# Constant loads of GpSimd begun behind the sixth K tile of the first weight block

## The chip, the cores and the metric

The kernel runs on one core of one Trainium2 chip. A core has a matrix engine (TensorE, PE in the profile), three other compute engines (VectorE = DVE, ScalarE = ACT, GpSimd = POOL), a queue engine (SyncE = SP) and 16 DMA engines that all queues share. SP, ACT and POOL can each start transfers; the profile lists what they issue under SPq, ACTq and POOLq, and the transfers themselves under queues q1 (SP), q10 (ACT) and q0 (POOL). The metric is the device time of one execution in microseconds; 2070.61 us is the median of three runs before the change (2067.7 to 2071.45).

## What is computed

Two layers over a sequence of 512 tokens with 2048 features, in float32. Each layer is x + W_out(mixer(RMSNorm(x)) * silu(gate)). The first mixer is gated differential attention with 8 heads, the second a gated RWKV-7 time mixing. Only the first layer's beginning matters here:

```python
hn = rms_norm(x, norm_w[0])
proj = hn @ w_in                                   # 2048 -> 4 * 2048
q, k, v, gate = jnp.split(proj, 4, axis=-1)
q = apply_rope(rms_norm(q, q_gain), cos, sin)      # cos, sin from positions and 64 frequencies
k = apply_rope(rms_norm(k, k_gain), cos, sin)
lam = exp(sum(lam_q1 * lam_k1)) - exp(sum(lam_q2 * lam_k2)) + lambda_init
o = causal_diff_attention(q, k, v, lam)
o = rms_norm(o, subln_w) * (1.0 - lambda_init)     # the output norm, its weights are "subw"
```

So the attention layer needs nine small constants beside its matrices: the positions, the 64 frequencies, two gains of 128, four lambda vectors of 128 and the output norm's 256 weights.

## The kernel before

A float32 product is made of three products of a faster 32-bit type. An operand a is split into hi (a rounded copy) and lo (a - hi), and a*b is hi*hi + hi*lo + lo*hi (`mm3`, L122). For weights ScalarE makes the hi part `wh` (L105) and VectorE the lo part `wl` (L106) of a tile `wraw` of two K tiles by 512 columns, 512 KB (`split_w`). For the input, ScalarE makes `hH` (L1110) and VectorE `hL` (L1111) of one K tile of x transposed, 256 KB, scaled with the norm weights (`make_h`). There are 16 K tiles of 128, so 8 weight tiles in a block of 512 columns.

The first weight block is the Q and K columns of head 0. `unit_tok` goes over its 8 weight tiles; for each it splits the weights, then the two tiles of x (`turn`, which appends the two instructions to `g.made`), and issues 24 products: 4 row tiles of 128 tokens, 2 K tiles, 3 products. Its raw weights have three buffers, wh and wl two each, so the cast of a weight tile waits until TensorE is done with the tile two before it. SP loads x tiles and weight tiles in one fixed order, each issue also waiting for the transfer eight issues before. Weights and x of K tiles 0 to 5 are issued ahead of everything. The second block is the V and gate columns of head 0 (`vg_cols`), with the same `unit_tok`.

Beside these products, VectorE and ScalarE do more: sums of the input tiles for later heads (`input_sums`, L497 to L521, also on tiles named pair), the squares of x for the norm (L888, from 1 MB loads that ScalarE issues at L882 once hH of K tiles 7, 10 and 15 is made), and the constants of the attention layer. The constants are made by `rope_tables` (L195 to L225: positions cast to float at L197, angles at L201, sine and cosine at L211 and L212, tables with the gains at L221 to L225), `lambda_full` (L234 to L243) and the two lines for `subw` (L905, L907). Their nine loads are issued by GpSimd. Each engine works its instructions off in order.

The order of the instructions on each engine is set by a scheduler of the language: it places them by data dependences, by priority (`high_priority`), and by explicit edges: `with tc.issue_after(ins)` puts instructions of the same engine behind `ins`. Before the change, rope_tables stands behind the split of the tenth K tile on ScalarE and VectorE (`g.made[9]`) and, on GpSimd, behind the causal mask (`masked`). So VectorE's and ScalarE's parts have their place in the middle of the first block, while GpSimd's loads start as soon as the mask is made.

Of the kernel before, what the change touches and what calls it, by code (L numbers as in the profile page):

```python
# [13 lines left out]
F32 = mybir.dt.float32  # L14
# [9 lines left out]
P = 128  # L24
# [221 lines left out]
def copy_out(g, dst, ps):  # L246
    with g.tc.high_priority(offset=AHEAD):
        for d, p in zip(dst, ps):
            m = g.nc.scalar.copy(d, p[:])
    return m.ins  # L250
# [562 lines left out]
def layer0(g, aps):  # L813
    nc, tc = g.nc, g.tc
    lx = ExitStack()
    g.lc = lx.enter_context(tc.tile_pool(name="lc0", bufs=1))
    with ExitStack() as cx:
# [56 lines left out]
        copied = copy_out(g, [t[:] for t in t1s], qk0)  # L874
        sc = g.work.tile([P, NT, 4], F32, name="ssc", tag="y", bufs=1)
        for cb, tags in enumerate((("qkL",), ("sA2",), ("sC2",), ("qkL",))):
# [8 lines left out]
            for t in range(NT):  # L885
                junk = g.work.tile([P, 512], F32, name="junkx", tag="al", bufs=1)
                with tc.issue_after(g.made[12 + t][0] if cb == 0 else copied):
# [8 lines left out]
        nc.gpsimd.memset(g.mask[:], 0.0)  # L896
        masked = nc.gpsimd.affine_select(out=g.mask[:], in_=g.mask[:], compare_op=ALU.is_ge, fill=NEG,
                                base=(NT - 1) * P, pattern=[[-1, T]], channel_multiplier=1).ins
        with tc.issue_after(g.made[9][0]), tc.issue_after(g.made[9][1]):
            with tc.issue_after(masked):  # L900
                rope_tables(g, aps)
        with tc.issue_after(copied), tc.issue_after(g.made[-1][1]), tc.issue_after(masked):
            lambda_full(g, aps)
        g.subw = g.lc.tile([P, 2], F32, name="subw")
        nc.gpsimd.dma_start(out=g.subw[:], in_=aps["da_subln_w"][0].rearrange("(c p) -> p c", p=P))  # L905
        with tc.issue_after(g.made[9][1]):
            nc.vector.tensor_scalar(g.subw[:], g.subw[:], 0.5 * (1.0 - LAMBDA_INIT), None, ALU.mult)  # L907
        before = None
        for h in range(NH):
# [850 lines left out]
@with_exitstack  # L1760
def body(ctx, tc, nc, aps):
    g = Ctx()
    g.nc, g.tc = nc, tc
    g.last, g.first, g.centred = None, [], None
    g.chains, g.later, g.state, g.copied = [], [], None, None
    g.const = ctx.enter_context(tc.tile_pool(name="const", bufs=1))
    g.hp = ctx.enter_context(tc.tile_pool(name="hp", bufs=16))
    g.wraw = ctx.enter_context(tc.tile_pool(name="wrawp", bufs=3))
    g.wh = ctx.enter_context(tc.tile_pool(name="whp", bufs=2))
    g.wl = ctx.enter_context(tc.tile_pool(name="wlp", bufs=2))  # L1770
    g.small = ctx.enter_context(tc.tile_pool(name="small", bufs=2))
    dr = ctx.enter_context(tc.tile_pool(name="dr", bufs=1, space=DRAM))
    g.ys = [dr.tile([D - 256, T], F32, name=f"ys{i}") for i in range(2)]
    g.yd2 = dr.tile([D, T], F32, name="yd2")
    g.xd = aps["x1"] if "x1" in aps else dr.tile([T, D], F32, name="xd")
    g.ltd = dr.tile([2, 2, 2, NC_, HALF + 1, HALF], F32, name="ltd")
    g.td = dr.tile([2, HALF // NG, P, HALF], F32, name="td")
    g.ident = g.const.tile([P, P], F32, name="ident")
    make_identity(nc, g.ident)
    for n, layer in ((4, layer0), (2, layer1)):  # L1780
        with tc.tile_pool(name="pp", bufs=n, space=PSUM) as g.pp, \
                tc.tile_pool(name="ps", bufs=1, space=PSUM) as g.ps:
            layer(g, aps)
# [41 lines left out]
```

## Time and profile before

| | |
|---|---|
| median of three runs | 2070.61 us (2067.7 to 2071.45) |
| profiled execution | 2071.26 us |
| its span | 2069.6 us |
| TensorE busy | 2050.2 us, 99% |
| VectorE busy | 1610.9 us, 78% |
| ScalarE busy | 1129.7 us, 55% |
| GpSimd busy | 389.0 us, 19% |
| DMA, whole span | 297.76 MB, 144 GB/s |

Times in the profile count from the span's start. A row of the timeline is start, length, engine, line, operation, out<-in, count, and in brackets how long the engine had been idle and what ended that. Issues of transfers have the engine's name with a q; what lands is seen where an engine stops waiting for it. Matmuls overlap: a product of 512 columns is shown 0.39 us long while the next one starts well before it ends. PEclk is the granted clock of TensorE as a share of full speed.

### The profile page before, as it was taken

The numbers are of one execution on the slowest core, as the hardware profiler recorded it, in microseconds if no ns is written. First come the engines' busy times: TensorE is split into PE (matmuls) and PEld (weight loads), VectorE is DVE, ScalarE is ACT, GpSimd is POOL, SyncE is SP. The second block draws the span as 40 slices with busy tenths as digits, with TensorE's granted clock in tenths as the row PEclk, the third lists the DMA queues.
The fourth block names the chain that finished last, engine by engine and source line by source line (L and its number), as shares of the span: only waits on it lengthen the run. The fifth ranks groups of instructions, "written<-read, shape, count | busy, mean of one in ns | idle before, by whom it ended". The sixth has DMA issues, their size and how long they took to land.

```text
span 2069.6 us, 34177 instructions
## 1 busy us (share of the span) xinstructions
PE 2050.2 (99%) x11936; PEld 1676.1 (81%) x11936; DVE 1610.9 (78%) x4121; ACT 1129.7 (55%) x2246; POOL 389.0 (19%) x773
## 2 busy tenths in 40 slices
PE   9999999999999999999999999999999999999999
PEld 7888888888888888888777778888888888877787
DVE  6988989888898976475778887877778878777755
ACT  4765666566665544345465555555555555545333
POOL 1010211102111100101122222222222222232011
PEclk9999999999999999999999999999999999999999
DMA  8487978879787965733323233233333332346676
GB/s 269 133 182 193 167 186 182 169 189 164 186 179 173 255 234 166 173 91 107 102 82 93 84 92 96 78 103 100 97 97 92 89 97 80 110 129 202 197 193 142
DMA packets 159533, 297.76 MB, mean 144 GB/s; under 512 B 64528, under 2 KB 81936, under 8 KB 159360
## 3 DMA queue, kind: packets, MB, share of 16 engines
q1 hardware_dynamic: 110768, 184.39, 28.6%
q0 software_dynamic: 25952, 90.88, 23.2%
q10 hardware_dynamic: 22640, 20.30, 3.0%
q8 instruction: 94, 1.54, 0.3%
q14 instruction: 79, 0.65, 0.1%
HBM read 271.33 MB, written 24.18 MB: 143 GB/s over the span
## 4 chain that ended last, share of the span: by engine, by line
PE 87%; DVE 8%; ACT 2%; issue 2%; DMA 2%; ACTq 0%; DVEq 0%; POOLq 0%; SPq 0%
PE pp L122 44%; PE pp L573 22%; PE pt L122 5%; DVE wl L106 2%; PE sm L1514 2%; PE gp L1324 1%; PE sc L122 1%; PE o L122 1%; PE sm L1532 1%; PE sm L1525 1%; PE lora L122 1%; PE z L122 1%; PE Y L1554 1%; ACT wh L105 1%; DMA wraw<-in_da_w_in_dram 1%
## 5 line engine op out<-in xcount | busy, mean ns | idle before, releaser
L106 DVE TENSOR_TENSOR wl<-wraw,wh 128x1024 fp32r<-128x1024 f32 (+2 forms) x290 | 355.2, 1225 | 180.5 <-ACT wh L105 175.5
L105 ACT CAST wh<-wraw 128x1024 fp32r<-128x1024 f32 (+2 forms) x290 | 302.6, 1043 | 260.5 <-PE pp L122 117.6
L122 PE MATMUL pp<-hL,wh 128*128 128x512 f32 x1024 | 414.2, 405 | 0.0
L122 PE MATMUL pp<-hH,wl 128*128 128x512 f32 x1024 | 413.0, 403 | 0.0
L122 PE MATMUL pp<-hH,wh 128*128 128x512 f32 x1024 | 412.7, 403 | 0.0
L122 PEld LDWEIGHTS pp<-hH,wh 128*128 128x128 f32 x1024 | 193.0, 189 | 34.7 <-issue 0.4
L122 PEld LDWEIGHTS pp<-hL,wh 128*128 128x128 f32 x1024 | 193.1, 189 | 33.7
L122 PEld LDWEIGHTS pp<-hH,wl 128*128 128x128 f32 x1024 | 193.3, 189 | 32.3
L573 PE MATMUL pp<-wh,hH 128*128 128x512 f32 x448 | 176.8, 395 | 0.0
L573 PE MATMUL pp<-wh,hL 128*128 128x512 f32 x448 | 175.8, 392 | 0.0
L122 PE MATMUL pp<-wh,hH 128*128 128x512 f32 x376 | 148.2, 395 | 1.9 <-ACT hH L1110 1.7
L122 PE MATMUL pp<-wh,hL 128*128 128x512 f32 x376 | 148.7, 395 | 0.3 <-DVE hL L1111 0.2
L122 PE MATMUL pp<-wl,hH 128*128 128x512 f32 x376 | 148.1, 394 | 0.7 <-DVE wl L106 0.5
L1383 DVE SCALAR_TENSOR_TENSOR tmpl<-LT,Tm 128x60 f32<-128x60 f32 (+24 forms) x496 | 134.1, 270 | 13.3
L573 PE MATMUL pp<-wl,hH 128*128 128x512 f32 x448 | 140.3, 392 | 0.0
L1520 POOL COPY SA<-VS 64x64 f32<-64x64 f32 x224 | 57.1, 255 | 401.7 <-DVE VS L1536 381.4
L1385 DVE TENSOR_TENSOR Tm<-Tm,tmpl 128x60 f32<-128x60 f32 (+24 forms) x496 | 104.0, 210 | 11.7
L1517 ACT COPY rhs<-sm 64x64 f32<-64x64 f32 x256 | 53.0, 207 | 91.2 <-PE sm L1514 88.7
L573 PEld LDWEIGHTS pp<-wl,hH 128*128 128x128 f32 x448 | 84.4, 188 | 17.2
L573 PEld LDWEIGHTS pp<-wh,hH 128*128 128x128 f32 x448 | 84.2, 188 | 17.2 <-issue 0.3
L573 PEld LDWEIGHTS pp<-wh,hL 128*128 128x128 f32 x448 | 84.2, 188 | 16.2
L1527 ACT COPY VS<-sm 64x64 f32<-64x64 f32 x256 | 52.9, 206 | 72.0 <-PE sm L1525 65.6
(403 smaller groups left out, 4381.8 us busy)
## 6 DMA issues: line engine op xcount, KB each, us to landing
wraw<-in_rw_w_in_dram SPq DMA_DIRECT2D x128, 512.0 KB
wraw<-in_da_w_in_dram SPq DMA_DIRECT2D x75, 512.0 KB
wraw<-in_da_w_in_dram POOLq DMA_DIRECT2D x28, 512.0 KB, 6.7
wraw<-in_da_w_out_dram SPq DMA_DIRECT2D x26, 512.0 KB
wraw<-in_rw_w_out_dram SPq DMA_DIRECT2D x24, 512.0 KB
Ta<-in_da_w_in_dram POOLq DMA_DIRECT2D x21, 512.0 KB, 5.8
Tb<-in_da_w_in_dram POOLq DMA_DIRECT2D x21, 512.0 KB, 5.8
Tc<-in_da_w_in_dram POOLq DMA_DIRECT2D x21, 512.0 KB, 5.5
```

Of the source, the lines that this page charges most:

```text
L105: a = nc.scalar.copy(hi[:, ks], raw[:, ks])
L106: d = nc.vector.tensor_sub(lo[:, ks], raw[:, ks], hi[:, ks].bitcast(F32))
L122: m = nc.tensor.matmul(out, a, b, start=s, stop=e, skip_group_check=skip)
L573: m = nc.tensor.matmul(out[t][:], x, wt[lo][:, k, :], start=first, stop=end and lo == 1 and k == KG - 1, skip_group_check=True)
L1324: m = nc.tensor.matmul(gp[h][:, i * P : (i + 1) * P], BK[r_, c0 + i, :, :], p.AR[r_, c0 + i, :, :], start=True, stop=True)
L1383: nc.vector.scalar_tensor_tensor(tt, LT[:, i : i + 1, i + 1 :].to_broadcast([P, s, n]), n2[:, i : i + 1], Tm[:, 0:s, i : i + 1].to_broadca ...
L1385: nc.vector.tensor_add(Tm[:, 0:s, i + 1 :], Tm[:, 0:s, i + 1 :], tt)
L1514: nc.tensor.matmul(sm[:, 0:P], both(p.G[:, c, 0]), both(VS[:, c]), start=True, stop=True)
L1517: nc.scalar.copy(rhs[r_, :], sm[r_, h * C : h * C + C])
L1520: nc.gpsimd.tensor_copy(p.SA[r_, c - 1, :], VS[r_, c, h, :])
L1525: nc.tensor.matmul(sm[:, P : P + C], both(g.TT[j % 2][:, c]), rhs[:], start=True, stop=True)
L1527: g.copied = nc.scalar.copy(VS[r_, c, h, :], sm[r_, P : P + C])
```

## The change

GpSimd gets one more instruction, a copy of one column of `hL[5]` into a small tile that nothing reads. hL[5] is the lo part of the sixth K tile, made by VectorE. The name `masked` now stands for this copy, so everything that stood behind the mask on GpSimd, which is the loads of rope_tables and of lambda_full, stands behind the copy; the load of the output norm's weights is put behind it too. The scale of those weights on VectorE (0.5 * (1 - lambda_init)) no longer stands behind K tile 9 but behind the last K tile.

```diff
         masked = nc.gpsimd.affine_select(out=g.mask[:], in_=g.mask[:], compare_op=ALU.is_ge, fill=NEG,
                                 base=(NT - 1) * P, pattern=[[-1, T]], channel_multiplier=1).ins
+        behind = g.small.tile([P, 1], F32, name="behind", tag="so")
+        with tc.issue_after(masked):
+            masked = nc.gpsimd.tensor_copy(behind[:], g.hL[5][:, 0:1].bitcast(F32)).ins
         with tc.issue_after(g.made[9][0]), tc.issue_after(g.made[9][1]):
             with tc.issue_after(masked):
                 rope_tables(g, aps)
         with tc.issue_after(copied), tc.issue_after(g.made[-1][1]), tc.issue_after(masked):
             lambda_full(g, aps)
         g.subw = g.lc.tile([P, 2], F32, name="subw")
-        nc.gpsimd.dma_start(out=g.subw[:], in_=aps["da_subln_w"][0].rearrange("(c p) -> p c", p=P))
-        with tc.issue_after(g.made[9][1]):
+        with tc.issue_after(masked):
+            nc.gpsimd.dma_start(out=g.subw[:], in_=aps["da_subln_w"][0].rearrange("(c p) -> p c", p=P))
+        with tc.issue_after(copied), tc.issue_after(g.made[-1][1]):
             nc.vector.tensor_scalar(g.subw[:], g.subw[:], 0.5 * (1.0 - LAMBDA_INIT), None, ALU.mult)
```

Line numbers behind the change are four higher from L899 on, so L1111 is L1115.

GpSimd's queue at the start of the program, before (the names: ident and mask are made on GpSimd itself, ropein holds the frequencies and the gains, lam the lambda vectors, Ta is the first accumulating weight load of head 1; in brackets the semaphores waited for):

```order
L897 AFFINE_SELECT mask<-mask 128x512 [waits Pool_49]
L195 DMA pos_i<-in_positions_dram 128x4x1
L199 DMA ropein<-in_inv_freq_dram 128x64
L219 DMA ropein<-in_da_q_gain_dram 128x128
L219 DMA ropein<-in_da_k_gain_dram 128x128
L234 DMA lam<-in_da_lam_q_dram 128x128
```

and now:

```order
L897 AFFINE_SELECT mask<-mask 128x512 [waits Pool_49]
L901 COPY behind<-hL 128x1 [waits DVE_49]
L195 DMA pos_i<-in_positions_dram 128x4x1
L199 DMA ropein<-in_inv_freq_dram 128x64
L219 DMA ropein<-in_da_q_gain_dram 128x128
L219 DMA ropein<-in_da_k_gain_dram 128x128
L234 DMA lam<-in_da_lam_q_dram 128x128
```

The loads keep their order; ahead of them there is now a copy that waits for VectorE.

VectorE behind K tiles 8 and 9 of the first block, before (hL here are those two tiles, pos is the cast of the positions):

```order
L106 TENSOR_TENSOR wl<-wraw,wh 128x1024
L1111 SCALAR_TENSOR_TENSOR hL<-pair,norms,hH 128x512 x2
L197 CAST pos<-pos_i 128x4
L907 TENSOR_SCALAR subw<-subw 128x2
L514 TENSOR_SCALAR pair<-pair,norms 128x256
L201 TENSOR_SCALAR rope<-ropein,pos 128x64 x4
```

and now:

```order
L106 TENSOR_TENSOR wl<-wraw,wh 128x1024
L1115 SCALAR_TENSOR_TENSOR hL<-pair,norms,hH 128x512 x2
L197 CAST pos<-pos_i 128x4
L514 TENSOR_SCALAR pair<-pair,norms 128x256
L201 TENSOR_SCALAR rope<-ropein,pos 128x64 x4
```

The two instructions that need the positions and the frequencies keep their place; the scale of subw has left it.

VectorE ahead of the split of the second weight tile of the V and gate block (the L106 row; L502, L514, L519 and L521 are input_sums), before:

```order
L519 SCALAR_TENSOR_TENSOR pair<-pair,norms 128x256
L521 TENSOR_TENSOR pair<-pair 128x256
L514 TENSOR_SCALAR pair<-pair,norms 128x256 x2
L502 SCALAR_TENSOR_TENSOR pair<-pair,norms 128x256 x2
L514 TENSOR_SCALAR pair<-pair,norms 128x256
L106 TENSOR_TENSOR wl<-wraw,wh 128x1024
L502 SCALAR_TENSOR_TENSOR pair<-pair,norms 128x256
L514 TENSOR_SCALAR pair<-pair,norms 128x256
```

and now:

```order
L519 SCALAR_TENSOR_TENSOR pair<-pair,norms 128x256
L521 TENSOR_TENSOR pair<-pair 128x256
L502 SCALAR_TENSOR_TENSOR pair<-pair,norms 128x256
L514 TENSOR_SCALAR pair<-pair,norms 128x256 x2
L502 SCALAR_TENSOR_TENSOR pair<-pair,norms 128x256 x2
L106 TENSOR_TENSOR wl<-wraw,wh 128x1024
L514 TENSOR_SCALAR pair<-pair,norms 128x256
L502 SCALAR_TENSOR_TENSOR pair<-pair,norms 128x256
```

Counted from the first block on, one L502 more stands ahead of this split. SP's order is the same in both kernels; TensorE's differs in the place of two groups of transposes in the second block by one product each; ScalarE's differs by a few instructions of input_sums and an earlier issue of one 32 KB load (mu).

## The prediction

> **What bounds the kernel now.** I read the page first, then the first 30 us in windows, then the chain of waits, then the DMA queues in two stretches. The profiled execution took 2071.26 us with a span of 2069.6 us, 0.65 us above the median of 2070.61 us, and the sum below is made against it.
>
> ```profile
> span 2069.6 us, 34177 instructions
> PE 2050.2 (99%) x11936; PEld 1676.1 (81%) x11936; DVE 1610.9 (78%) x4121; ACT 1129.7 (55%) x2246; POOL 389.0 (19%) x773
> ```
>
> TensorE is busy 99% of the span. A gap of TensorE that closes is therefore worth its length, wherever it lies, provided that nothing opens behind it. The change touches the first weight block, so its gaps are looked at there. Columns: stretch and its length, busy us of each engine, granted TensorE clock, DMA share, GB/s.
>
> ```profile
> 0.00:5.00 5.00, 3.10 (x14) 3.11 (x15) 0.06 (x1) 1.87 (x3) 4.31 (x13) 1.00 0.60 182
> 5.00:10.00 5.00, 4.87 (x22) 3.75 (x21) 2.80 (x5) 3.00 (x5) 2.74 (x5) 1.00 1.03 288
> 10.00:15.00 5.00, 4.80 (x18) 2.85 (x17) 2.73 (x3) 1.58 (x3) 0.00 (x0) 1.00 0.95 132
> 15.00:20.00 5.00, 4.38 (x19) 3.26 (x18) 0.00 (x0) 0.63 (x1) 0.00 (x0) 1.00 0.89 233
> 20.00:25.00 5.00, 3.61 (x10) 2.43 (x11) 3.09 (x4) 3.26 (x6) 0.00 (x0) 0.83 1.02 397
> ```
>
> From 10 to 20 us the DMA engines are busy nine tenths of the time and yet move 132 and 233 GB/s, where the next stretch moves 397. The chain of waits says who suffers:
>
> ```profile
> 4.78 14.49 DMA wraw<-in_da_w_in_dram
> 19.37 1.05 ACT wh L105
> ```
>
> The weight tile of K tiles 4 and 5 is issued at 4.78 us and lands only at 19.3 us. The DMA queues tell why: first the stretch 7 to 19 us, then 19.4 to 37 us (q0 is GpSimd's queue, q1 SP's, q10 ScalarE's; last the share of 16 engines' time).
>
> ```profile
> DMA packets 1047, 2.15 MB, mean 179 GB/s; under 512 B 241, under 2 KB 241, under 8 KB 1047
> ...
> q0 software_dynamic: 265, 0.43, 49.7%
> q1 hardware_dynamic: 782, 1.72, 43.5%
> ...
> DMA packets 2716, 6.54 MB, mean 372 GB/s; under 512 B 270, under 2 KB 270, under 8 KB 2715
> ...
> q1 hardware_dynamic: 2132, 5.39, 79.2%
> q10 hardware_dynamic: 572, 1.14, 19.7%
> ```
>
> GpSimd's nine constant loads bring 0.43 MB and hold half of the DMA engines' time for 12 us, 6.0 us of all sixteen; SP's stream brings 1.72 MB in the remaining 43.5%, at 330 GB/s of its own time. Those 6.0 us stand ahead of a tile that TensorE waits for.
>
> **The change, part by part.** TensorE's own rows give what can be won (the first row is ScalarE's, ahead of the first product). Columns: start, length, engine, line, operation, count, and in brackets the idle time before it.
>
> ```profile
> 5.76 0.72 ACT L1110 ACTIVATE hH<-pair,norms 128x512 fp32r<-128x512 f32 x1 [0.54 <-DMA norms<-in_norm_w_dram]
> ...
> 12.23 0.39 PE L122 MATMUL pp<-wh,hL 128*128 128x512 f32 x1
> 15.11 0.39 PE L122 MATMUL pp<-wh,hH 128*128 128x512 f32 x1
> 18.99 0.39 PE L122 MATMUL pp<-wh,hL 128*128 128x512 f32 x1
> 21.09 0.49 PE L122 MATMUL pp<-wh,hH 128*128 128x512 f32 x1 [1.71 <-ACT hH L1110]
> 29.15 0.39 PE L122 MATMUL pp<-wh,hH 128*128 128x512 f32 x1
> ```
> ```profile
> 23.50:26.50 3.00, 3.00 (x9) 2.34 (x8) 0.50 1.03 400
> 12.71:21.09 8.38, 6.57 (x25) 4.27 (x25) 1.00 0.93 234
> 21.09:29.15 8.06, 7.76 (x25) 5.74 (x25) 0.79 1.03 397
> ```
>
> Each pair of K tiles is 24 products (4 row tiles, 2 K tiles, 3 products). Undisturbed they follow each other every 0.228 us: 17 steps from 15.11 to 18.99. A pair is then 5.47 us. The last product of the first pair starts at 12.23, so the second pair could start at 12.46, the third at 17.93 and the fourth at 23.40. They start at 12.71, 21.09 and 29.15. The loss is 0.25 us before the second pair, 8.38 - 5.47 = 2.91 in it, and 8.06 - 5.47 = 2.59 in the third, 5.75 us together. Of the 2.59 about 1.5 come from the granted clock, 0.50 in the window 23.5 to 26.5: at half clock three microseconds do the work of one and a half.
>
> (a) Removed from the start: the nine loads. With 6.0 us of engine time gone, the tile of K tiles 4 and 5 lands at 13.3 us at the latest (19.3 - 6.0; SP's rate left as it is). At the earliest, with 0.91 MB moved by 5 us (182 GB/s) and 372 GB/s after that, the 2.62 MB up to this tile (4 x tiles of 256 KB, 3 weight tiles of 512 KB) are there at 5 + 1.71/0.372 = 9.6 us. Either will do: ScalarE's cast cannot begin before 12.5, when TensorE gives the weight buffer of the first pair back, and even 13.3 leaves the third pair four microseconds. I take the whole 5.75 us; the lower bound is 4.2, if the slow clock of 1.5 us stays, and the upper 6.3, if the norm weights, for which the first split waits 0.54 us, come that much sooner.
>
> (b) Moved: the nine loads begin behind hL[5]. GpSimd's queue holds nothing else before the accumulating loads of L86 at 110 us, so all that waits behind the new copy are the loads themselves; who waits for them is VectorE, at four places.
>
> ```profile
> 2.36 0.93 POOL L195 DMA_DIRECT2D pos_i<-in_positions_dram  x1
> 3.28 0.57 POOL L199 DMA_DIRECT2D ropein<-in_inv_freq_dram  x1
> 19.37 1.04 ACT L105 CAST wh<-wraw 128x1024 fp32r<-128x1024 f32 x1 [5.43 <-DMA wraw<-in_da_w_in_dram]
> 21.59 1.41 DVE L1111 SCALAR_TENSOR_TENSOR hL<-pair,norms,hH 128x512 fp32r<-128x512 f32 x2
> 30.43 1.22 DVE L106 TENSOR_TENSOR wl<-wraw,wh 128x1024 fp32r<-128x1024 f32 x1 [3.42 <-ACT wh L105]
> 33.30 0.74 DVE L201 TENSOR_SCALAR rope<-ropein,pos 128x64 f32<-128x64 f32 x4
> ```
> ```profile
> ropein<-in_inv_freq_dram POOLq DMA_DIRECT2D x1, 32.0 KB, 6.1
> pos_i<-in_positions_dram POOLq DMA_DIRECT2D x1, 2.0 KB, 6.4
> lam<-in_da_lam_k_dram POOLq DMA_DIRECT2D x2, 64.0 KB, 12.4
> subw<-in_da_subln_w_dram POOLq DMA_DIRECT2D x1, 1.0 KB, 11.6
> L1520 POOL COPY SA<-VS 64x64 f32<-64x64 f32 x224 | 57.1, 255 | 401.7 <-DVE VS L1536 381.4
> ```
>
> From cast to the end of hL[5] is 3.63 us (19.37 to 23.00), so hL[5] is done at 16.1 to 16.9. GpSimd's copy of one column is not in the trace; its nearest row, 64x64, takes 0.26 us, and between nothing and twice that it does not matter. The frequencies landed 7.0 us after the first issue began (0.92 to their own issue, then 6.1): now at 23.4 to 24.2. VectorE wants them at L201, which moves from 33.30 to 27.6, since VectorE's work there hangs on TensorE freeing a weight buffer (the cast behind the third pair). Margin 3.4 us or more, cost nothing. With the landing of the slowest quoted load, 12.4 us, they would come at 29.7 to 30.5, 2.9 us late at most: the lower end. The gains, lambda and norm weights are wanted 9 us and more after L201 and issue within 5 us, so they are covered.
>
> (c) Reordered: VectorE is full from 30 us to 62 us, and TensorE meets that once.
>
> ```profile
> 58.32 0.48 DVE L502 SCALAR_TENSOR_TENSOR pair<-pair,minus 128x256 f32<-128x256 f32 x1
> 58.72 0.47 DVE L502 SCALAR_TENSOR_TENSOR pair<-pair,norms 128x256 f32<-128x256 f32 x1
> 62.69 0.50 PE L122 MATMUL pp<-wl,hH 128*128 128x512 f32 x1 [0.52 <-DVE wl L106]
> ```
>
> Ahead of that split (the second weight tile of the V and gate columns) the new order has one L502 more, 0.47 us in its row, of which some 0.07 overlap the next instruction (two in a row start 0.40 apart); the norm's scale L907 stays ahead of it, only later. So the wait of 0.52 becomes 0.92. Bounds: 0.40, and nothing if VectorE's own small idles swallow it. I take 0.40.
>
> The sum: 5.75 - 0 - 0.40 = 5.35 us. The profiled execution would be 2065.9 us, the median 2070.61 - 5.35 = 2065.3 us.
>
> A rule weighed against this. The DMA engines' time is only moved, and SP and ScalarE still load in the new place. By the windows, GpSimd's packets held 50% of the engines whoever else had work, so I expect the same near 17 to 29 us. The Trainium skill, "DMA: Bandwidth & Descriptors", Queues, rings and completion order, says that each engine takes packets in turn from every queue that has work; the trace agrees with its 49.7% to 43.5%. By that rule a third queue, ScalarE's, cuts SP's turn from a half to a third and the sum would be 3.7 (the first rival has its working); by the rows alone SP keeps its rate and the sum is 5.35.
>
> **The rivals.**
> 1. The contention comes back later. Through K tile 11 SP must bring 6.8 MB (12 x tiles, 7 weight tiles, one of them for the next head). By 17.5 us it has 0.91 + 12.5 x 0.372 = 5.56 MB. The remaining 1.24 MB at 1.72 MB in 12 us take 8.7 us, to 26.2; the cast wants the tile at 23.40 + 5.47 = 28.9. If SP gets two thirds of that rate because ScalarE's 1 MB load takes its turn too, they take 13 us, to 30.5: 1.6 us late, gain 3.7, 2066.9 us. Against it: every load after that has still more time.
> 2. The slow clock stays, from a cause other than the gap before it: gain 5.35 - 1.5 = 3.9, 2066.8 us. For it: the trace shows the drop once in this block, after the gap, and so cannot tell the two apart.
> 3. The tile's lateness is not GpSimd's doing, and the engines stay slow for SP without it: gain 0 to 1, 2070 us. Against it: the rate rises to 372 GB/s just when q0 ends.
> 4. Slower: the frequencies come so late that VectorE, in order, stands at L197 or L201 with the split of the next pair behind it. VectorE has no slack to 62 us, so each microsecond late is one lost. From 5.35 us late the gain is gone, at 9.5 us it is 4.1 us slower; that is a landing of 19 us or more after issue, half again the longest quoted (12.4). If three queues in turn stretch the 12.4 by a half twice over, 28 us, the time is 2070.6 + 12 = 2083 us; I use 2076 for a milder case.
>
> **How the numbers follow.** Forecast 66%; rival 1 10%; rival 2 8%; rival 3 8%; rival 4 8%. The time is the forecast's, 2065.3 us; its own range is 2063.3 (the upper 6.3, the 0.40 not paid, and a microsecond of scatter between runs) to 2066.9. The 8 in 10 range goes up to 2070.5, which takes in rivals 1, 2 and 3 and leaves out rival 4 and the low end. About 0.2%, 4.1 us, is what a measurement of this kernel can tell from no change; the forecast lies 1.2 us beyond it, so some of its chance falls within. Faster by over 0.2% (below 2066.5): 55 of the 66 and 3 of rivals 1 and 2, 58%. Within: 34%. Slower: 8%.
>
> **What would show it.** (a) holds if no row of GpSimd's queue stands in 5 to 16 us, the rate there is near 370 GB/s, the third pair's first product starts near 18 us, and the fourth's near 23.4. The granted clock should stay 1.00 through 20 to 30 us. (b) holds if VectorE has no wait on a DMA at L197 and L201. (c) is right if TensorE's wait in the V and gate block is near 0.9 us. From 110 us on every stage should have its old length, moved by five microseconds. The prediction is wrong if ScalarE still waits for the weights of K tiles 4 and 5, if TensorE waits for those of 10 and 11, or if VectorE stands before the rotary tables.

## The result and the profile after

The changed kernel took 2065.84 us (median of 22 runs, 2064.72 to 2069.03), the kernel before on the same chip 2069.11 us (22 runs, 2067.65 to 2071.45). The ratio is 0.9983 with a 95% interval of 0.9977 to 0.9989: 0.17% less, 2.3 to 4.8 us. The interval lies wholly below 1, but the size is within the 0.2% that the prediction set as its bound. The profiled execution took 2065.33 us with a span of 2063.6 us, 5.9 us less than the profiled execution of before by time and 6.0 by span. So two profiles differ by more than the medians do, which is taken up below.

The head of the page, after:

```profile
span 2063.6 us, 34178 instructions
PE 2046.9 (99%) x11936; PEld 1676.1 (81%) x11936; DVE 1611.3 (78%) x4121; ACT 1128.4 (55%) x2246; POOL 388.6 (19%) x774
```

GpSimd has one instruction more, the new copy; the work of the others is what it was. The first stretches in windows, after (stretch and its length, busy us of TensorE, its weight loads, VectorE, ScalarE and GpSimd with their instructions, granted clock, DMA share, GB/s):

```profile
5.00:10.00 5.00, 5.00 (x23) 4.02 (x22) 3.63 (x6) 3.78 (x7) 0.00 (x0) 1.00 1.03 399
10.00:15.00 5.00, 5.00 (x24) 4.15 (x23) 3.20 (x5) 2.66 (x4) 0.00 (x0) 1.00 1.05 399
15.00:20.00 5.00, 5.00 (x24) 4.14 (x23) 2.11 (x3) 2.13 (x3) 3.87 (x8) 1.00 1.02 398
20.00:25.00 5.00, 5.00 (x24) 4.15 (x23) 2.11 (x4) 1.85 (x4) 1.64 (x3) 1.00 1.10 284
25.00:30.00 5.00, 5.00 (x24) 4.14 (x23) 5.00 (x17) 2.22 (x4) 0.00 (x0) 1.00 0.93 242
```

From 10 to 20 us the DMA engines are as busy as before, and move 399 and 398 GB/s where they moved 132 and 233. TensorE has no idle time from 5 to 30 us, and its granted clock stays 1.00. (The DMA share adds up the times of the packets as they are recorded, and so it can pass 1.00.) The low rate has moved with the loads: it stands at 20 to 30 us, 284 and 242. The DMA queues say the same, in the same two stretches as shown of before (7 to 19 us, then 19.4 to 37 us; q0 is GpSimd's queue, q1 SP's, q10 ScalarE's):

```profile
DMA packets 1994, 4.79 MB, mean 399 GB/s; under 512 B 223, under 2 KB 223, under 8 KB 1994
q1 hardware_dynamic: 1994, 4.79, 104.2%
...
DMA packets 2383, 5.27 MB, mean 299 GB/s; under 512 B 334, under 2 KB 334, under 8 KB 2381
q1 hardware_dynamic: 1055, 2.75, 43.8%
q10 hardware_dynamic: 1038, 2.06, 33.8%
q0 software_dynamic: 288, 0.43, 18.3%
```

From 7 to 19 us SP's queue alone brings 4.79 MB, where it had brought 1.72. In their new place the nine loads hold the engines for 18.3% of 17.6 us, which is 3.2 us; at the start they had held them for 6.0. Of the instructions, after (start, length, engine, line, operation, count, and in brackets the idle time before it with what ended it):

```profile
6.33 0.59 PE L122 MATMUL pp<-wh,hH 128*128 128x512 f32 x1
12.43 1.05 ACT L105 CAST wh<-wraw 128x1024 fp32r<-128x1024 f32 x1 [2.06 <-PE pp L122]
17.87 1.05 ACT L105 CAST wh<-wraw 128x1024 fp32r<-128x1024 f32 x1 [3.15 <-PE pp L122]
23.31 1.05 ACT L105 CAST wh<-wraw 128x1024 fp32r<-128x1024 f32 x1 [3.15 <-PE pp L122]
56.98 0.50 PE L122 MATMUL pp<-wl,hH 128*128 128x512 f32 x1 [0.85 <-DVE wl L106]
...
16.13 0.18 POOL L901 COPY behind<-hL 128x1 f32<-128x1 f32 x1 [13.73 <-DVE hL L1115]
16.25 0.93 POOL L195 DMA_DIRECT2D pos_i<-in_positions_dram  x1
26.86 0.16 DVE L197 CAST pos<-pos_i 128x4 f32<-128x4 int32 x1
27.20 0.74 DVE L201 TENSOR_SCALAR rope<-ropein,pos 128x64 f32<-128x64 f32 x4
```

The casts of the third, fourth and fifth weight tile come 5.44 us apart, and each waits for TensorE to give its buffer back and no longer for a transfer. TensorE's first wait after its first product is the one at 56.98. L197 and L201 carry no wait on a DMA. The landings, after (KB each, median us from issue to landing):

```profile
ropein<-in_inv_freq_dram POOLq DMA_DIRECT2D x1, 32.0 KB, 5.2
pos_i<-in_positions_dram POOLq DMA_DIRECT2D x1, 2.0 KB, 5.5
subw<-in_da_subln_w_dram POOLq DMA_DIRECT2D x1, 1.0 KB, 9.2
lam<-in_da_lam_k_dram POOLq DMA_DIRECT2D x2, 64.0 KB, 8.5
```

Each is shorter than before, although three queues now have work at once.

### The profile page after: what moved, and what is told of

Its sections match the earlier page's. It is cut to its first block, busy times and chain, and to the rows that moved or that the text cites. A ratio compares the mean times of both kernels' runs of the same rounds, so it can differ in the third digit from the quotient of the medians.

```text
span 2063.6 us, 34178 instructions
## 1 busy us (share of the span) xinstructions
PE 2046.9 (99%) x11936; PEld 1676.1 (81%) x11936; DVE 1611.3 (78%) x4121; ACT 1128.4 (55%) x2246; POOL 388.6 (19%) x774
## 4 chain that ended last, share of the span: by engine, by line
PE 89%; DVE 7%; ACT 2%; issue 1%; DMA 1%; ACTq 0%; POOL 0%; DVEq 0%; SPq 0%; POOLq 0%
PE pp L122 44%; PE pp L573 24%; PE pt L122 5%; PE sm L1518 2%; DVE wl L106 1%; PE gp L1328 1%; PE sc L122 1%; PE o L122 1%; PE sm L1536 1%; PE sm L1529 1%; PE lora L122 1%; PE z L122 1%; DVE tmpl L1387 1%; PE Y L1558 1%; PE pt L296 1%
## 5 line engine op out<-in xcount | busy, mean ns | idle before, releaser
L106 DVE TENSOR_TENSOR wl<-wraw,wh 128x1024 fp32r<-128x1024 f32 (+2 forms) x290 | 354.6, 1223 | 179.1 <-ACT wh L105 174.1
```

The lines of the kernel that those rows point to most:

```text
L106: d = nc.vector.tensor_sub(lo[:, ks], raw[:, ks], hi[:, ks].bitcast(F32))
```

## The experiments

The theory was the prediction's: nine loads at the start hold the DMA engines for 6 us, the third weight tile is late by that, and TensorE loses its time there. The main rivals: that the order on VectorE does it, that the place behind the sixth K tile matters, and that the loads' cost lies in a few of them. All times are compared with the kernel before on the same chip: 2069.64 us (33 runs) beside the first four kernels, 2070.19 (25 runs) beside the next three. The other four runs are single executions, read for their profiles.

### The two halves of the change

The first kernel moves the loads and leaves the output norm's scale where it was on VectorE. Against the changed kernel:

```diff
-        with tc.issue_after(copied), tc.issue_after(g.made[-1][1]):
+        with tc.issue_after(g.made[9][1]):
             nc.vector.tensor_scalar(g.subw[:], g.subw[:], 0.5 * (1.0 - LAMBDA_INIT), None, ALU.mult)
```

> The loads begin behind the sixth K tile as in the change, but the scale of the output norm's weights stays behind K tile 9; VectorE's order is then the order of before. In the profile after the change the load of these weights is issued at 22.0 us (it waits for the positions) and lands 9.2 us later, at 31.2, while VectorE comes to this place at 26.9 us. My theory (VectorE is full up to the second weight tile of the V and gate block, so that every wait there reaches TensorE): VectorE stands about 4.3 us at the scale, TensorE's wait in the V and gate block grows from 0.8 to 4.5 to 5 us, and the time is back within 1 us of before (0.9996 to 1.0004 of it). Rival (VectorE has slack to swallow it): TensorE's wait stays under 1.5 us and the time is that of the change, 0.9983.

It took 2069.07 us (11 runs), ratio 0.9994 (0.9985 to 1.0003), span 2067.4: 3.8 us more than the changed kernel's span. The timeline of this kernel:

```profile
31.13 0.17 DVE L911 TENSOR_SCALAR subw<-subw 128x2 f32<-128x2 f32 x1 [3.90 <-DMA subw<-in_da_subln_w_dram]
59.87 0.50 PE L122 MATMUL pp<-wl,hH 128*128 128x512 f32 x1 [1.29 <-DVE wl L106]
```

VectorE stands 3.90 us for the norm weights, the last of the nine loads, and the product of the V and gate columns that was at 56.98 comes at 59.87. The theory held in the sum: the time is back within 1 us of the kernel before. It had the wait at that product in one piece, 4.5 to 5 us, and there it was wrong: TensorE's row shows 1.29 us, and the rest of the 2.9 us lies earlier (39 products from 30 to 40 us, where the changed kernel has 46). The span is longer by another 0.9 us behind this product, which is no more than what lies behind the first block scatters by from one execution to the next (see the size, below). The scale's place is thus part of what makes the change worth anything: without it the moved loads bring nothing that these runs can tell from no change.

The second kernel does only the other half: loads at the start, the scale later. Against the kernel before:

```diff
-        with tc.issue_after(g.made[9][1]):
+        with tc.issue_after(copied), tc.issue_after(g.made[-1][1]):
             nc.vector.tensor_scalar(g.subw[:], g.subw[:], 0.5 * (1.0 - LAMBDA_INIT), None, ALU.mult)
```

> The loads stay at the start, only the scale moves behind the last K tile; VectorE's, ScalarE's and TensorE's orders are those of the change. Theory (the gain is the DMA engines' time): the third weight tile still lands near 19 us, the third pair starts near 21 us, TensorE's wait in the V and gate block is 0.8 to 0.9 us, the time that of before to 0.4 us more (1.0000 to 1.0002). Rival (the new order of VectorE brings the gain): 0.9983.

It took 2070.45 us (11 runs), ratio 1.0002 (0.9993 to 1.0012), span 2069.1. Its windows and its timeline:

```profile
10.00:15.00 5.00, 4.38 (x19) 3.01 (x18) 2.58 (x3) 1.43 (x2) 0.00 (x0) 1.00 0.94 91
20.00:25.00 5.00, 3.12 (x11) 2.09 (x12) 2.56 (x4) 3.25 (x5) 0.00 (x0) 1.00 1.03 391
...
19.87 1.04 ACT L105 CAST wh<-wraw 128x1024 fp32r<-128x1024 f32 x1 [6.07 <-DMA wraw<-in_da_w_in_dram]
21.59 0.50 PE L122 MATMUL pp<-wh,hH 128*128 128x512 f32 x1 [2.35 <-ACT hH L1110]
61.91 0.50 PE L122 MATMUL pp<-wl,hH 128*128 128x512 f32 x1 [0.86 <-DVE wl L106]
```

The engines execute in the changed kernel's order, and the third weight tile is as late as before: order alone gains nothing, as the theory had it. The wait at the V and gate columns is 0.86 us, as in the changed kernel (0.85) and not as in the one before (0.52), so this wait comes with the new order and not with the loads. And in this profile the granted clock stays 1.00 behind a gap of 2.35 us, where in the profile of before it fell behind one of 1.71.

### Where the loads begin

Two kernels move only the point behind which the loads are issued, to the second and to the tenth K tile. Against the changed kernel, the line of the one and the line of the other:

```diff
-            masked = nc.gpsimd.tensor_copy(behind[:], g.hL[5][:, 0:1].bitcast(F32)).ins
+            masked = nc.gpsimd.tensor_copy(behind[:], g.hL[1][:, 0:1].bitcast(F32)).ins
...
+            masked = nc.gpsimd.tensor_copy(behind[:], g.hL[9][:, 0:1].bitcast(F32)).ins
```

> As the change, but the loads begin behind hL of the second K tile instead of the sixth; all orders are otherwise the same. hL[1] is done at 8.3 us, so GpSimd's packets are on the DMA engines from about 9.5 to 20 us. By 9.3 us the 2.62 MB up to the third weight tile have landed at the rate after the change. Theory (what counts is only that the loads stay off the DMA engines until this tile is in): the third pair starts at 18 to 19 us, the tiles after it land late but ahead of their use, time within 0.5 us of the change (0.9981 to 0.9986). Rival (contention at any time in the first 20 us costs its share): the third or fourth pair starts late by 2 us or more and half of the gain is gone, 0.9990 to 0.9995.

It took 2065.74 us (11 runs), ratio 0.9982 (0.9973 to 0.9990). Windows and timeline, loads behind the second K tile:

```profile
15.00:20.00 5.00, 5.00 (x24) 4.14 (x23) 2.11 (x3) 1.98 (x3) 0.68 (x1) 1.00 1.08 190
...
12.58 1.05 ACT L105 CAST wh<-wraw 128x1024 fp32r<-128x1024 f32 x1 [2.00 <-PE pp L122]
18.02 1.05 ACT L105 CAST wh<-wraw 128x1024 fp32r<-128x1024 f32 x1 [3.15 <-PE pp L122]
```

The rate falls to 190 GB/s at 15 to 20 us, less than the 233 of the kernel before, and costs nothing, as the theory had it: by then the third tile is in, and the fourth is cast at 18.02 us as soon as TensorE gives its buffer back. The low rate is a cost only where a tile is due.

> As the change, but behind hL of the tenth K tile, done at 26.9 us; the scheduler puts the positions' cast and the angles some instructions later on VectorE. Positions land near 32.6, frequencies near 33.3 us. Theory (VectorE's waits reach TensorE one to one): VectorE stands 2 to 4 us in all at these two, TensorE's wait in the V and gate block grows to 3 to 5 us, and most of the gain is gone, 0.9993 to 1.0000. Rival (only the start matters): 0.9983.

It took 2065.40 us (11 runs), ratio 0.9980 (0.9971 to 0.9989). This is a miss: a smaller gain or none was expected, from VectorE standing at the rotary tables. Timeline and landings, loads behind the tenth K tile:

```profile
30.11 0.26 DVE L197 CAST pos<-pos_i 128x4 f32<-128x4 int32 x1 [0.44 <-DMA pos_i<-in_positions_dram]
...
ropein<-in_inv_freq_dram POOLq DMA_DIRECT2D x1, 32.0 KB, 4.1
pos_i<-in_positions_dram POOLq DMA_DIRECT2D x1, 2.0 KB, 2.8
```

The first of them is issued at 27.29 us, and VectorE waits 0.44 us. Two things were not reckoned with. The positions land in 2.8 us and the frequencies in 4.1, not in 5.5 and 5.2. And the scheduler, which orders VectorE's instructions when the kernel is built, put L197 and L201 later; the expectation had named that, but not how far L201 moved, behind the twelfth K tile's split. With that order the wait at the V and gate columns (0.85) is gone too. So this kernel changes the order besides the place. It cannot be told apart from the change: at the three places tried, behind the second, the sixth and the tenth K tile, the loads gain the same within the noise.

### Which loads cost

The next three split or enlarge the group at the start. The first keeps the seven loads that spread one row over 128 partitions (the frequencies, two gains, four of lambda) at the start and moves only the two loads of 4-byte elements (positions, norm weights). Its core, against the changed kernel:

```diff
-    nc.gpsimd.dma_start(out=pos_i[:], in_=aps["positions"].rearrange("o (t p) -> (o p) t", p=P),)
+    with g.tc.issue_after(g.behind):
+        nc.gpsimd.dma_start(out=pos_i[:], in_=aps["positions"].rearrange("o (t p) -> (o p) t", p=P),)
...
-            masked = nc.gpsimd.tensor_copy(behind[:], g.hL[5][:, 0:1].bitcast(F32)).ins
+            g.behind = nc.gpsimd.tensor_copy(behind[:], g.hL[5][:, 0:1].bitcast(F32)).ins
...
-        with tc.issue_after(masked):
+        with tc.issue_after(g.behind):
             nc.gpsimd.dma_start(out=g.subw[:], in_=aps["da_subln_w"][0].rearrange("(c p) -> p c", p=P))
```

> As the change, but only the two loads of single elements (positions, 512 of 4 bytes; output norm's weights, 256 of 4 bytes) begin behind the sixth K tile; the seven broadcasts of a row over 128 partitions (896 rows of 256 or 512 bytes, 0.43 MB) load from the start. Theory (the broadcasts hold the DMA engines): the third weight tile lands at 17 to 19.5 us, the third pair starts after 19.5 us, and the time is near before, 0.9992 to 1.0002. Rival (the time goes by the number of elements and rows, 896 to 768): the tile lands near 16.5 us, the third pair starts at about 18, and the time is near the change, 0.9981 to 0.9988.

It took 2070.06 us (10 runs), ratio 1.0000 (0.9991 to 1.0010). The queues from 5 to 19 us, a window, and the timeline:

```profile
q1 hardware_dynamic: 1099, 2.59, 58.1%
q0 software_dynamic: 224, 0.43, 37.0%
...
15.00:20.00 5.00, 4.33 (x12) 3.17 (x13) 1.39 (x2) 1.96 (x3) 0.00 (x0) 0.73 0.87 250
...
18.28 1.04 ACT L105 CAST wh<-wraw 128x1024 fp32r<-128x1024 f32 x1 [2.72 <-DMA wraw<-in_da_w_in_dram]
```

The seven spread loads hold 37.0% of 14 us, 5.2 us of all sixteen engines, and the third tile is late again. The theory held. In this profile the clock falls already from 15 to 20 us, behind a gap of 2.38 us that TensorE has within the second pair of K tiles.

The other way round, the two loads of 4-byte elements stay at the start and the seven move. The core, against the changed kernel, with these two loads taken out of their old places:

```diff
+        with tc.issue_after(masked):
+            nc.gpsimd.dma_start(out=g.pos_i[:], in_=aps["positions"].rearrange("o (t p) -> (o p) t", p=P),)
+            nc.gpsimd.dma_start(out=g.subw[:], in_=aps["da_subln_w"][0].rearrange("(c p) -> p c", p=P))
         behind = g.small.tile([P, 1], F32, name="behind", tag="so")
```

> The counterpart: the seven broadcasts begin behind the sixth K tile, positions and output norm's weights load from the start. Theory (broadcasts): the third tile lands by 13 us, no wait of ScalarE for it beyond TensorE's, time that of the change, 0.9980 to 0.9986. Rival (number of elements and rows): GpSimd's queue holds the engines for some 2.8 us ahead of this tile, which lands near 15 us; still early enough for TensorE, so the time says nothing, but the DMA rate in 5 to 10 us is well under 399 GB/s.

It took 2067.10 us (10 runs), ratio 0.9985 (0.9975 to 0.9994). The queues from 5 to 19 us, and the timeline:

```profile
q0 software_dynamic: 64, 0.00, 8.0%
q1 hardware_dynamic: 2111, 4.96, 93.5%
...
12.56 1.06 ACT L105 CAST wh<-wraw 128x1024 fp32r<-128x1024 f32 x1 [1.02 <-PE pp L122]
```

The two small loads, 3 KB together, still hold 8.0% of 14 us, 1.1 us. The rate from 5 to 10 us is 272 GB/s where the changed kernel has 399, a sign that the expectation had given to its rival, so they are not free. But the third tile is there in time, and the gain is that of the change within both intervals. The seven spread loads are what costs TensorE its time.

Then more of the same: the kernel before with four more such loads at the start, into a tile that nothing reads.

```diff
+        more = g.work.tile([P, 4, P], F32, name="more", tag="al", bufs=1)
+        for i in range(4):
+            nc.gpsimd.dma_start(out=more[:, i], in_=aps["da_q_gain"][0].partition_broadcast(P))
```

> The kernel before with four more broadcasts of one row of 128 numbers (0.26 MB) ahead of the nine loads, into a tile that nothing reads. Theory (GpSimd's loads hold 6.0 us of the engines for 0.43 MB): four more hold 3.7 us; the third weight tile lands near 23 us, the third pair starts 3 to 4 us later than before's 21.1, and the time is 1.0012 to 1.0022. Rival (the tile is late for another reason): the time is that of before within 0.5 us.

It took 2074.26 us (10 runs), ratio 1.0018 (1.0009 to 1.0027), span 2072.6. The queues from 5 to 19 us, a window, and the timeline:

```profile
q0 software_dynamic: 308, 0.49, 57.7%
q1 hardware_dynamic: 815, 2.02, 40.7%
...
15.00:20.00 5.00, 4.24 (x11) 2.76 (x12) 1.50 (x2) 1.32 (x2) 0.55 (x2) 0.77 1.00 138
...
21.08 1.05 ACT L105 CAST wh<-wraw 128x1024 fp32r<-128x1024 f32 x1 [4.38 <-DMA wraw<-in_da_w_in_dram]
```

GpSimd's queue holds 8.1 us of these 14, and the kernel is slower by about as much as the change is faster. The time held; the place only in part: the third tile is cast at 21.08 and not near 23. Some of the loss lies ahead of it: the second half of the first weight tile is cast at 8.86 us where the kernel before has 6.39, and TensorE stands 2.15 us ahead of the second pair.

The last of this kind asks whether it is the form of the loads or GpSimd's queue. The seven spread loads go out at the start from ScalarE's queue; the two small ones stay. The core, against the kernel before, with the loads taken out of the two functions:

```diff
+            for dst, src in ((g.rows[:, 2, 0:64], aps["inv_freq"]), (g.rows[:, 0], aps["da_q_gain"][0]),
...
+                with tc.issue_after(first):
+                    first = nc.scalar.dma_start(out=dst, in_=src.partition_broadcast(P)).ins
```

> The kernel before, but the seven broadcasts are issued from ScalarE's queue at the start instead of GpSimd's (positions and output norm's weights stay with GpSimd). Its time is not to be compared, since SP's issues then share their waits with seven more transfers; what is read is the share of the DMA engines that the queues hold from 5 to 19 us. Theory (the form of the transfer is dear, one source row written 128 times): the broadcasts on q10 hold the engines for about as long as they did on GpSimd's queue, some 5 us of sixteen for 0.43 MB, so 30% or more, and SP's rate stays under 270 GB/s. Rival (GpSimd's queue is dear): they hold under 15% and SP runs near 350 GB/s.

Its profile has a span of 2065.9 us (one execution). The queues from 5 to 19 us:

```profile
q1 hardware_dynamic: 1355, 3.19, 65.7%
q10 hardware_dynamic: 1007, 0.42, 25.0%
q0 software_dynamic: 64, 0.00, 4.7%
```

For 0.42 MB the engines are held 25.0% of 14 us, 3.5 us, against 5.2 us from GpSimd's queue. That lies between the 30% and the 15% of the two explanations; SP's rate, 3.19 MB in 14 us or 228 GB/s, is what the form was expected to give (under 270) and far from the other (350). That the queue counts is not shown by this: from GpSimd's own queue the same seven loads held the engines for 3.2 us (18.1% of 19.4 to 37 us) when they began behind the sixth K tile. So the time that these loads hold the engines goes by when they run, and the part of the queue stays open.

### The size: more profiles of the same two kernels

The kernel before was profiled twice more, and the changed one once.

> The kernel before, unchanged, profiled again. In its first profile TensorE's granted clock was 0.50 from 23.5 to 26.5 us, which cost 1.5 us; in the run with the scale alone moved it was 1.00 in the same stretch, though TensorE had stood idle for 2.4 us in one piece just before. Theory (the drop belongs to some executions only, and this is why the profile of before lies 2 us above the median and the medians differ by less than the profiles): the clock here may be 1.00 throughout 20 to 30 us, with a span 1.5 us shorter than 2069.6. Rival (the gap of TensorE brings the drop each time): 0.50 for about 3 us again.

> The kernel before, profiled a third time. The two profiles so far differ in the first block alone: the cast of the fifth weight tile starts at 29.3 and at 26.4 us, the spans are 2069.6 and 2066.8. Theory (an execution's time goes by how the loads fall in this block, and by the clock drop): cast of the fifth tile and span lie on the same line, span = cast + 2040.3 within 0.7 us. Rival (other stages scatter as much): off the line by more than 1.5 us.

> The changed kernel, profiled again. Theory: its first block has nothing left to scatter, the cast of the fifth weight tile starts at 23.3 us again to 0.3, the clock is 1.00 through 30 us. Rival: the clock drops in some executions of this kernel as well, and the cast is 1.5 us later.

The cast of the fifth weight tile is the mark: behind it all kernels have the same work left, up to the few tenths at the V and gate columns. From the timelines: the kernel before, first, second and third profile, then the changed kernel's second.

```profile
29.34 1.05 ACT L105 CAST wh<-wraw 128x1024 fp32r<-128x1024 f32 x1 [3.68 <-PE pp L122]
```
```profile
26.40 1.05 ACT L105 CAST wh<-wraw 128x1024 fp32r<-128x1024 f32 x1 [1.05 <-PE pp L122]
```
```profile
28.37 1.06 ACT L105 CAST wh<-wraw 128x1024 fp32r<-128x1024 f32 x1 [3.33 <-PE pp L122]
```
```profile
23.43 1.06 ACT L105 CAST wh<-wraw 128x1024 fp32r<-128x1024 f32 x1 [3.15 <-PE pp L122]
```

And the stretch 20 to 25 us in windows, second and third profile of before:

```profile
20.00:25.00 5.00, 4.66 (x19) 3.49 (x20) 2.29 (x3) 2.86 (x5) 0.00 (x0) 1.00 1.04 405
```
```profile
20.00:25.00 5.00, 4.55 (x12) 3.16 (x13) 3.22 (x5) 2.96 (x5) 0.00 (x0) 0.74 1.04 406
```

The spans are 2069.6, 2066.8 and 2069.5 us for before, 2063.6 and 2064.6 for after. The start of the changed kernel repeats within 0.12 us (23.31, 23.43). That of the kernel before does not: 29.34, 26.40, 28.37, and with it goes the clock, low in the first and third profile and full in the second. Span less cast is 2040.3, 2040.4 and 2041.1 for before, 2040.3 and 2041.2 for after: what lies behind these tiles scatters by 0.9 us in these five, and a difference between the two kernels does not stand out of it. For the third profile of before a distance of at most 0.7 us from 2040.3 was expected, and 0.8 was measured; for the changed kernel the expectation held.

The later stages can scatter more. The profile with the seven loads alone moved has no loss in the first block (fifth cast at 23.44), and yet its span is 2066.2 us, 2042.8 more than the cast. (The profile that keeps the seven lies as far off, 2070.9 less 28.09, without a clock drop behind the cast.) With the seven moved the clock falls at 1880 us, far behind this block, after a TensorE wait of 1.10 us:

```profile
1880.00:1882.00 2.00, 2.00 (x7) 1.58 (x6) 2.00 (x7) 1.92 (x5) 0.00 (x0) 0.60 1.06 310
```

How often the clock falls is seen from the mean granted clock that every run lists: 1.5 us lost of 2070 are 0.07%, so by this estimate one drop shows as 0.999. With the spread loads at the start the mean is below 1.00 in 52 of 89 runs (31 of 58 of the kernel before, 6 of 11 with the scale alone moved, 5 of 10 with the seven kept, all 10 with four more). With these loads later it is in 7 of 65: 4 of the changed kernel's 22, and 3 of the 43 of the four kernels with the scale early, behind the second and the tenth K tile, and with the seven alone moved. The four of the changed kernel have a median of 2068.02 us, its other 18 one of 2065.40. So a drop is more frequent with the loads at the start, but they do not bring it each time, and it is not gone without them.

## Why the prediction was right, point by point

**What bounds.** Right. TensorE is 99% busy in both, and what the kernels above gain or lose beyond the scatter was found in the first five weight tiles, and with the early scale in the stall behind them.

**(a) The nine loads.** The mechanism held at each place. Nothing of GpSimd's queue moves between 7 and 19 us, the rate there is 399 GB/s, the third pair's cast comes at 12.43 and the others at 17.87 and 23.31, where 12.5, 17.93 and 23.40 were given for the pairs. Moving the seven spread loads alone gives the gain, keeping them alone takes it away, and four more cost about as much again. What was mis-sized is this term's 5.75 us, taken whole. It was read from one execution of the kernel before, in which the start was the slowest of the three that were profiled. Against the mark of the changed kernel's first profile (23.31) the three profiles of before lose 6.0, 3.1 and 5.1 us in the first block, 4.7 in the mean. With the 0.33 us of (c) off that is 4.4 us, in the upper part of the measured 2.3 to 4.8. The runs say so without the mark. Among those with a mean clock of 1.00 beside the first four kernels the median of before is 2068.59 us (17 runs), with the loads behind the second and the tenth K tile 2065.74 and 2065.40: 2.9 and 3.2 us less, where the prediction without its clock term had 5.75 - 1.5 - 0.40 = 3.85. One profile of before cannot show this. The three runs given with it could have warned: the lowest, 2067.7, lies 2.9 us under their median.

**The 1.5 us of slow clock in (a).** They went when the gap went, as forecast, in both profiles of the changed kernel. They were counted as there in every execution of before, and were there in two of three profiles; by the mean clock of the runs in about half. Nor are they always gone: 4 of the changed kernel's 22 runs list 0.999, where in the execution is not known. What sets the drop is open. The gap's length alone does not: 2.35 us in the kernel with only the scale moved left the clock at 1.00, 2.38 in the kernel that keeps the seven loads did not. The Trainium skill, "TensorE: Matmul & The Clock Gate", What's actually happening, says that activity is judged in windows of about 3.4 us that run freely, whatever the kernel does; by that, the same gap would cost clock in one execution and not in the next, which agrees with two drops in three profiles. But it names an idle window as the cause, and the gaps here, 1.71 us in the row of the first profile, are shorter than one; no run here shows the windows.

**(b) The moved loads.** Right: hL[5] is done at 16.1, and L201 runs at 27.20 (27.6 was given) without a wait. The frequencies land in 5.2 us instead of the 6.1 to 12.4 that were taken as bounds, so the margin is larger than was reckoned.

**(c) The order on VectorE.** Right: 0.85 us for the forecast 0.92. The kernel with the old loads and the new order shows 0.86, so that term is shown by itself.

**The rivals.** The first, contention that comes back, is half true: SP's share does fall to 43.8%, with three queues at work, and its rate with it. But no cast waits for a weight tile; the slack was there. Nor do GpSimd's packets hold half of the engines again near 17 to 29 us, as was expected: they hold 25.6% of that stretch. The rule of the Trainium skill weighed in the prediction ("DMA: Bandwidth & Descriptors", Queues, rings and completion order) is not contradicted by the shares 43.8, 33.8 and 18.3%, but not shown by them either, since the three queues need not have had work all the time. The sum of 3.7 us that went with it is close to what was measured by chance: it rested on a late tile, and there is none. The second, a slow clock that stays, did not come in either profile, 1.00 throughout; by the four runs named above it cannot be shut out for every execution. The third, that the tile's lateness is not GpSimd's doing, is out by the kernels that split the loads. The fourth, VectorE standing, did not happen in the change, but its mechanism is real: with the scale left early, VectorE stood for 3.90 us and the product of the V and gate columns came 2.9 us later.

**The time.** 2065.3 us was forecast and 2065.84 measured, within the range and the likeliest case's own. That it came so near is in part luck. The forecast took 5.35 us off 2070.61 us, the median of three runs; over 22 runs the kernel before takes 2069.11, 1.5 us less, and the gain is 3.27 us, 2.1 less and with an interval that does not reach 5.35. The two errors offset each other. Since the gain is 0.17%, it falls in "same" by the prediction's bound, which had 34%, and not in "faster by over 0.2%", which had 58%; by the sign of the interval it is faster.

## What to carry to other kernels

Small loads that spread a row over all partitions are not small for the DMA engines: keep them off until the tiles are in that the busiest engine waits for next. After that the place hardly mattered here, but an in-order engine that consumes the last of them must have its consumer moved too, or the gain is lost there. And a gap that comes from transfers in competition changed here from one execution to the next: size it from several profiles, not from one, and take the time to start from out of many runs.

## What was not expected of the hardware

- Seven loads of 0.42 MB hold the sixteen DMA engines for 5.2 us from GpSimd's queue at the start, for 3.5 us from ScalarE's there, and for 3.2 us from GpSimd's queue behind the sixth K tile: some 80, 120 and 130 GB/s while they hold them, where SP's tiles alone move at 399 GB/s. All nine held them for 3.2 us behind the sixth K tile and for 6.1 behind the tenth (40.9% of 27 to 42 us). Two loads, together 3 KB, of 4-byte elements hold them for 1.1 us.
- The same 2 KB of positions land in 6.4 us when they are issued at the start, 6.0 behind the second K tile, 5.5 behind the sixth and 2.8 behind the tenth. What sets this was not tested.
- The granted clock falls to about half for some 3 us in some executions of one and the same kernel and not in others: by the mean clock in 31 of 58 runs of the kernel before and 4 of 22 of the changed one.
